# Which two of three accumulator banks share a PSUM tile: the up projection's units of seven in a hybrid transformer layer

## The chip, the core and the metric

The kernel runs on one core of a Trainium2 chip. It computes one layer of a diffusion backbone in fp32, with matrix products made of three products of rounded parts (`fp32r`). The metric is the device time of one execution in microseconds; the numbers of a kernel are the median of its runs, and one further execution is taken by the profiler.

Engines are named as the profile names them: PE is TensorE (matmuls; PEld is its weight load), DVE is VectorE, ACT is ScalarE, POOL is GpSimd, SP the queue that issues most DMAs.

## The reference

The layer is adaLN modulation, neighbourhood attention and bidirectional retention, a merge, an output projection, and then an MLP with a depthwise convolution over tokens. The change lies in the MLP's first half:

```python
def _conv_ffn(h, w_up, conv_w, conv_b, w_down):
    u = h @ w_up                                   # (1024, 1024) @ (1024, 5632)
    up = jnp.pad(u, ((0, 0), (pad, pad), (0, 0)))
    u = sum(up[:, i:i + n] * conv_w[i] for i in range(CONV_W)) + conv_b
    a, val = jnp.split(u, 2, axis=-1)
    return (jax.nn.silu(a) * val) @ w_down
```

`w_up` has 2 x 2816 columns: a gate half and a value half, each in 22 blocks of 128. A block `j` of the gate and block `j` of the value belong together, since they meet in `silu(a) * val`.

## The kernel before

**The units.** The up projection goes block by block in 22 units. The first two are plain: eight products of 128 columns by 512 tokens for gate and value. The other twenty are units of seven (class `Up`, a `Seven`): gate and value block are the two rows of a 2 x 2 block matrix, the two halves of the input features its columns, and the input `h` is split likewise into two feature halves and two token halves, B11, B21, B12, B22. Seven products in place of eight then give the four results (gate or value, token half); for that, weights are summed beforehand (`load`, four sums on POOL, L1401 to L1404) and inputs too (T1 to T4, ready in SBUF). A product is twelve matmuls of 128x512 (`prod`, L1387): four feature blocks by the three combinations of rounded high and low parts. Before it, ACT rounds the weight (L1412) and DVE makes the low part (L1413).

Each unit accumulates in three banks of PSUM, X, Y and Z, 512 fp32 columns each:

| step | input | bank | after it |
|---|---|---|---|
| 0 | B11 (`h2a`) | X, opened | p1 = copy of X, ACT, L1433 |
| 1 | T2 | Y, opened | u2 = Y + p1, DVE, L1436 |
| 2 | T1 | Z, opened | |
| 3 | T3 | Y, added to | u3 = Y + p1, DVE, L1442; then the add of result (1,1) = Z + u3, DVE, L1423 |
| 4 | B21 (`h2a`) | X, added to | result (0,0) = copy of X, ACT, L1851 |
| 5 | T4 | Y, added to | the add of result (1,0) = Y + p1, DVE, L1423 |
| 6 | B22 (`h2h`, `h2l`) | Z, added to | the add of result (0,1) = Z + u2, DVE, L1423; then the unit's convolution |

The convolution (`conv`) of a unit has for gate (`ta`) and value (`at`) a scaled copy on ACT (L1784) and two taps on DVE (L1785, L1786), then silu (L1787, ACT) and a product (L1788, DVE). For every second unit POOL then makes four sums of its outputs (L1802).

**The tiles.** `u_tile` gives a PSUM tile of two banks. There are two pools of two such tiles; the units use the pools in turn, and a unit takes both tiles of its pool. Of its four banks it uses three: before the change X and Y are the two halves of the first tile, and Z is the first half of the second. The kernel is written in a framework that adds the waits between engines itself, from the tiles that each instruction reads and writes, and that may put a ready instruction ahead of its place in the program.

**The order.** Two units are always under way. `interleaved` sorts the steps by

```python
sorted((7 * i + 2 * k, i, k) for i in range(n0, n) for k in range(7))
```

so that between two steps of a unit there is one of its neighbour, and a unit starts just ahead of its predecessor's step 4: (i, 3), (i+1, 0), (i, 4), (i+1, 1), (i, 5), (i+1, 2), (i, 6), (i+1, 3), (i+2, 0), (i+1, 4) and so on. In the first unit of seven, which has no predecessor of its kind, steps 1 and 2 stand in exchanged order before the change. PE and DVE each work through one queue in order.

After the up projection follows the down projection (matmuls of `y` on line 1387), with the tile framework again moving a few of its first matmuls into the end of the stage.

Of the kernel before, what the change touches and what calls it, by code (L numbers as in the profile page):

```python
# [32 lines left out]
NF = FF // P  # L33
# [7 lines left out]
def tile_hybrid_layer(ctx, tc: tile.TileContext, io, dbg=None):  # L41
# [1417 lines left out]
    def interleaved(n0, n):  # L1459
        return [(i, k) for _, i, k in sorted((7 * i + 2 * k, i, k) for i in range(n0, n) for k in range(7))]  # L1460

    class Gates(Seven):
# [17 lines left out]
        def banks(self):  # L1480
            self.X, self.Y, self.Z = (g_ps("u") for _ in range(3))
# [30 lines left out]
    for db in range(KB):  # L1512
# [5 lines left out]
        for half in range(2):  # L1518
# [6 lines left out]
            t = onap.tile([P, 512], F32, tag="pn", bufs=3, name="pnt")  # L1525
# [120 lines left out]
    for kb in range(KB):  # L1646
        t = wop.tile([P, 2, 512], F32R, tag="wo", bufs=KB, name="wo")
# [11 lines left out]
    for kb in (6, 7, 0, 1, 2, 3, 4, 5):  # L1659
        t = (wop if kb >= 6 else op).tile([P, 2, 512], F32R, tag="wx", bufs=2, name="wx") if kb >= 4 else None  # L1660
# [73 lines left out]
    def u_tile(n):  # L1734
        return pu[n // 2 % 2].tile([P, T], F32, tag="u", bufs=2, name="u")
# [70 lines left out]
    def u_out():  # L1806
        return tap.tile([P, T], F32, tag="uu", bufs=4, name="uu")
# [13 lines left out]
    class Up(Seven):  # L1821
# [11 lines left out]

        def banks(self):
            t = u_tile(2 * self.n)
            self.X, self.Y = t[:, 0:512], t[:, 512:1024]
            self.Z = u_tile(2 * self.n + 1)[:, 0:512]
            self.u = [u_out() for _ in range(2)]

        def moving(self, c):  # L1840
# [27 lines left out]
    PLAIN = 2  # L1868
# [11 lines left out]
            combs[f"T{c + 1}"] = comb(c)  # L1880
        conv(j, *us2)
    units[PLAIN + 1].load()
    ups = interleaved(PLAIN, NF)
    ups[1:3] = ups[2], ups[1]
    for i, n in ups:
        units[i].step(n)
    pu[1].release()
    pu[0].release()
# [231 lines left out]
def build(nc, arrays):  # L2120
    io = {k: nc.dram_tensor(f"in_{k}", a.shape, mybir.dt.from_np(a.dtype), kind="ExternalInput").ap() for k, a in arrays.items()}
    io["out"] = nc.dram_tensor("out_0_dram", (T, D), F32, kind="ExternalOutput").ap()
    with tile.TileContext(nc) as tc:
        tile_hybrid_layer(tc, io)
# [11 lines left out]
```

## Time and profile before

| | |
|---|---|
| runs | 1733.86, 1733.59, 1732.75 us: median 1733.59 |
| profiled execution | 1731.98 us, of it 1729.9 us span from the first to the last instruction |
| granted PE clock over the span | 0.999 |
| PE, DVE, ACT, POOL busy, share of the span | 98%, 75%, 49%, 30% |
| units of seven | from 1126.4 to 1513.2 us of the span |
| matmuls in them | 1680 (20 units of 7 products of 12) |

How to read it. A row of the timeline gives the start in us from the span's start, the length in us, engine, line, operation, what it writes and reads, shape and count (rows of equal instructions that follow each other are merged). A matmul is listed with 0.39 us, but matmuls are pipelined and start at a closer pitch, so an engine row of PE that is busy all the time may still hide lost time: the pitch tells. An entry `a <- b: 3.7, 9, 0.6` of the waits says that `a` stood idle for 3.7 us in all, nine times, at most 0.6, until `b` was done. A row of the busy times by stretch has the stretch, its length, then busy time and count of PE, PEld, DVE, ACT and POOL, the clock, and the share and rate of the DMAs.

### The profile page before, as it was taken

What the parts mean: (1) busy time and instruction counts of PE and PEld (TensorE: products, weight loads), DVE (VectorE), ACT (ScalarE), POOL (GpSimd) and SP (SyncE); (2) the same over time, 40 slices, a digit from 0 to 9 for tenths busy, and PEclk for the clock granted to TensorE, in tenths of its full rate; (3) what the DMA queues carried; (4) which work ended last, traced back from release to release, by engine and by line L of the source; (5) the groups of instructions that cost most, each with busy time, mean ns of one, the idle gap of its engine ahead of it and who ended that gap; (6) DMA issues with size and microseconds to landing.
All of it is one profiled execution on the core that took longest, in us unless ns stands there. A gap on an engine that the chain in (4) does not pass through costs nothing.

```text
span 1729.9 us, 24670 instructions
## 1 busy us (share of the span) xinstructions
PE 1701.1 (98%) x8318; PEld 1416.1 (82%) x8318; DVE 1296.3 (75%) x2502; ACT 842.0 (49%) x1794; POOL 523.0 (30%) x443
## 2 busy tenths in 40 slices
PE   7999999999999999999999999999999999999998
PEld 4888888888888888888888888888888888888886
DVE  6578887766777776887665557888998998875757
ACT  7656666553353434544443333644444444554444
POOL 2100000002334243055413300265555555211444
PEclk9999999999999999999999999999999999999999
DMA  9243344343342323668568633732233332586754
GB/s 353 89 132 115 110 128 132 120 146 96 92 122 67 101 64 97 209 230 270 187 219 286 220 139 137 267 112 96 92 94 119 118 96 92 181 293 193 241 156 177
DMA packets 157998, 267.66 MB, mean 155 GB/s; under 512 B 26064, under 2 KB 46768, under 8 KB 157872
## 3 DMA queue, kind: packets, MB, share of 16 engines
q1 hardware_dynamic: 139952, 245.12, 43.5%
q10 hardware_dynamic: 17920, 20.98, 3.4%
q8 instruction: 65, 1.06, 0.3%
q14 instruction: 61, 0.50, 0.1%
HBM read 191.80 MB, written 71.61 MB: 152 GB/s over the span
## 4 chain that ended last, share of the span: by engine, by line
PE 46%; issue 5%; DVE 5%; POOL 3%; ACT 1%; DMA 1%; POOLq 0%; SPq 0%; ACTq 0%; DVEq 0%
PE u L1387 26%; PE y L1387 6%; PE pr L113 2%; PE pr L114 2%; PE pr L112 2%; PE om L124 1%; PE om L123 1%; PE om L125 1%; DVE wc L1413 1%; PE pn L114 1%; PE pn L112 1%; PE pn L113 1%; PE u L113 1%; PE u L114 1%; PE u L112 1%
## 5 line engine op out<-in xcount | busy, mean ns | idle before, releaser
L1387 PE MATMUL u<-T,wc 128*128 128x512 f32 x960 | 225.7, 391 | 0.5 <-ACT pu L1433 0.3
L1387 PEld LDWEIGHTS u<-T,wc 128*128 128x128 f32 x960 | 179.4, 188 | 41.2 <-ACT pu L1433 3.7
L1387 PE MATMUL y<-wc,ahl 128*128 128x512 f32 x924 | 210.1, 389 | 0.4 <-DVE wc L89 0.4
L1387 PEld LDWEIGHTS y<-wc,ahl 128*128 128x128 f32 x924 | 173.4, 188 | 36.8 <-DVE wc L89 0.8
L113 PE MATMUL mm<-low,wc 128*128 128x512 f32 (+1 forms) x320 | 121.4, 379 | 0.0
L1387 PE MATMUL u<-h2a,wc 128*128 128x512 f32 x480 | 112.8, 390 | 0.9 <-DVE pu L1442 0.8
L89 DVE TENSOR_TENSOR wc<-ur,wc 128x512 fp32r<-128x512 f32 x77 | 63.3, 823 | 61.4 <-ACT wc L88 61.4
L1387 PEld LDWEIGHTS u<-h2a,wc 128*128 128x128 f32 x480 | 90.0, 188 | 20.3 <-DVE pu L1442 1.2
L112 PE MATMUL mm<-hx,wc 128*128 128x512 f32 x256 | 103.8, 405 | 0.0
L114 PE MATMUL mm<-hx,wc 128*128 128x512 f32 x256 | 102.9, 402 | 0.0
L1412 ACT CAST wc<-s 128x512 fp32r<-128x512 f32 x80 | 49.7, 622 | 91.0 <-PE u L1387 88.8
L125 PE MATMUL mm<-wc,low 128*128 128x512 f32 (+1 forms) x240 | 91.4, 381 | 0.0
L1387 PE MATMUL u<-hxT,wc 128*128 128x512 f32 x384 | 89.6, 389 | 0.0
L1539 POOL TENSOR_TENSOR col<-col,bcol 128x32 f32<-128x32 f32 x1 | 0.3, 252 | 291.4 <-issue 291.4
L88 ACT CAST wc<-ur 128x512 fp32r<-128x512 f32 x77 | 47.8, 620 | 79.5 <-PE y L1387 74.5
L1413 DVE TENSOR_TENSOR wc<-s,wc 128x512 fp32r<-128x512 f32 x80 | 84.8, 1060 | 1.0 <-ACT wc L1412 0.6
L1387 PEld LDWEIGHTS u<-hxT,wc 128*128 128x128 f32 x384 | 72.1, 188 | 15.0
L89 DVE TENSOR_TENSOR wc<-raw,wc 128x512 fp32r<-128x512 f32 x93 | 63.6, 691 | 22.8 <-ACT wc L88 22.4
L88 ACT CAST wc<-raw 128x512 fp32r<-128x512 f32 x93 | 57.2, 620 | 46.7 <-DMA raw<-in_w_pret 7.7
L123 PE MATMUL mm<-wc,hx 128*128 128x512 f32 x192 | 75.2, 392 | 0.6 <-ACT r L1088 0.6
L124 PE MATMUL mm<-wc,hx 128*128 128x512 f32 x192 | 75.2, 392 | 0.0
L1413 DVE TENSOR_TENSOR wc<-wr,wc 128x512 fp32r<-128x512 f32 x55 | 55.0, 1006 | 17.6 <-ACT wc L1412 15.5
(397 smaller groups left out, 4711.1 us busy)
## 6 DMA issues: line engine op xcount, KB each, us to landing
ur<-in_w_up SPq DMA_DIRECT2D x80, 256.0 KB
ur<-d_a SPq DMA_DIRECT2D x77, 256.0 KB
aw<-in_w_ada SPq DMA_DIRECT2D x32, 512.0 KB
pj<-in_w_down SPq DMA_DIRECT2D x44, 256.0 KB
d_w<-pj SPq DMA_DIRECT2D x44, 256.0 KB
d_a<-sa SPq DMA_DIRECT2D x44, 256.0 KB
ur<-d_w SPq DMA_DIRECT2D x44, 256.0 KB
d_a<-at SPq DMA_DIRECT2D x33, 256.0 KB
```

Source lines behind the costliest of these rows:

```text
L88: act.copy(hi, src)
L89: (lo_eng or vec).tensor_tensor(lo, src, hi.bitcast(F32), ALU.subtract)
L112: pe.matmul(out, wh, xh, start=k == 0, stop=False)
L113: pe.matmul(out, wh, xl, start=False, stop=False)
L114: pe.matmul(out, wl, xh, start=False, stop=k == n - 1)
L123: pe.matmul(out, ah, bh, start=first, stop=False)
L124: pe.matmul(out, ah, bl, start=False, stop=False)
L125: pe.matmul(out, al, bh, start=False, stop=last)
L1387: pe.matmul(out, a, b, start=first and n == 0, stop=last and n == 2, skip_group_check=True)
L1412: pin(act.copy(w[:, 0], a))
L1413: pin(vec.tensor_tensor(w[:, 1], a, w[:, 0].bitcast(F32), ALU.subtract))
L1539: pool.tensor_tensor(col[:, 16:48], col[:, 16:48], bcol[:, 16:48], ALU.add)
```

## The change

X and Z now share the first tile of a unit, and Y has the second, alone. The first unit of seven takes its steps in the plain order of `interleaved`. Steps, products, sums and DMAs are the same in number and size.

```diff
         def banks(self):
             t = u_tile(2 * self.n)
-            self.X, self.Y = t[:, 0:512], t[:, 512:1024]
-            self.Z = u_tile(2 * self.n + 1)[:, 0:512]
+            self.X, self.Z = t[:, 0:512], t[:, 512:1024]
+            self.Y = u_tile(2 * self.n + 1)[:, 0:512]
             self.u = [u_out() for _ in range(2)]
...
     units[PLAIN + 1].load()
-    ups = interleaved(PLAIN, NF)
-    ups[1:3] = ups[2], ups[1]
-    for i, n in ups:
+    for i, n in interleaved(PLAIN, NF):
         units[i].step(n)
```

PE's queue, where one unit (first tile 12756) is about to take step 4 and the next (first tile 12902) has begun. The rows with 12909 as weight are step 0 of the next unit, those with 12925 step 4 of this one, those with T10 and T11 the start of step 1 of the next. Before:

```order
L1387 MATMUL u_12902<-h2a_11094,wc_12909 128x512 x3
L1387 MATMUL u_12902<-h2a_11095,wc_12909 128x512 x3
L1387 MATMUL u_12756<-h2a_11096,wc_12925 128x512 x3
L1387 MATMUL u_12756<-h2a_11097,wc_12925 128x512 x3
L1387 MATMUL u_12756<-h2a_11098,wc_12925 128x512 x3
L1387 MATMUL u_12756<-h2a_11099,wc_12925 128x512 x3
L1387 MATMUL u_12902<-T10_12147,wc_12941 128x512
L1387 MATMUL u_12902<-T11_12148,wc_12941 128x512
```

The same place with the change:

```order
L1387 MATMUL u_12902<-h2a_11094,wc_12909 128x512 x3
L1387 MATMUL u_12902<-h2a_11095,wc_12909 128x512 x3
L1387 MATMUL u_12903<-T10_12147,wc_12941 128x512
L1387 MATMUL u_12903<-T11_12148,wc_12941 128x512
L1387 MATMUL u_12903<-T10_12147,wc_12941 128x512
L1387 MATMUL u_12756<-h2a_11096,wc_12925 128x512 x3
L1387 MATMUL u_12756<-h2a_11097,wc_12925 128x512 x3
L1387 MATMUL u_12756<-h2a_11098,wc_12925 128x512 x3
L1387 MATMUL u_12756<-h2a_11099,wc_12925 128x512 x3
L1387 MATMUL u_12903<-T10_12147,wc_12941 128x512
L1387 MATMUL u_12903<-T11_12148,wc_12941 128x512
```

Three matmuls of the next unit's step 1 have come ahead of this unit's step 4; the other nine follow it. Step 1 writes a tile of its own now (12903), where it wrote the tile of step 0 (12902). It is so in seventeen of the twenty units.

DVE's queue at the same place, as a difference (rows without a sign are the same in both). The first row is the previous unit's last add, L1442 is u3 of this unit, and the last row the add of its result (1,1):

```order
-L1423 TENSOR_TENSOR uu_12599<-u_12598,pu_12602 128x512
+L1423 TENSOR_TENSOR uu_12599<-u_12597,pu_12602 128x512
 L1413 TENSOR_TENSOR wc_12973<-s_12894,wc_12973 128x512
 L1785 SCALAR_TENSOR_TENSOR ta_12859<-uu_12599,cw_12079,ta_12859 128x1023
-L1442 TENSOR_TENSOR pu_12762<-u_12756,pu_12760 128x512
+L1442 TENSOR_TENSOR pu_12762<-u_12757,pu_12760 128x512
 L1786 SCALAR_TENSOR_TENSOR ta_12859<-uu_12599,cw_12079,ta_12859 128x1023
-L1423 TENSOR_TENSOR uu_12759<-u_12757,pu_12762 128x512
+L1423 TENSOR_TENSOR uu_12759<-u_12756,pu_12762 128x512
```

DVE's order does not change, only the tiles that it reads: of the tile 12756, which step 4 writes, the reader was u3 (L1442) and is now the add two places behind it (L1423).

## The prediction

> **What bounds the kernel now.** I read the page first: busy times, then the chain that ended last.
>
> ```profile
> span 1729.9 us, 24670 instructions
> PE 1701.1 (98%) x8318; PEld 1416.1 (82%) x8318; DVE 1296.3 (75%) x2502; ACT 842.0 (49%) x1794; POOL 523.0 (30%) x443
> PE u L1387 26%; PE y L1387 6%; PE pr L113 2%; PE pr L114 2%; PE pr L112 2%; PE om L124 1%; PE om L123 1%; PE om L125 1%; DVE wc L1413 1%; PE pn L114 1%; PE pn L112 1%; PE pn L113 1%; PE u L113 1%; PE u L114 1%; PE u L112 1%
> ```
>
> TensorE bounds it, and its largest piece of the chain is the u products of line 1387. Time can be lost or won only where PE stands still there. For the stage of the units of seven I took the busy times of that stretch, and then its waits.
>
> ```profile
> 1126.30:1513.50 387.20, 385.82 (x1691) 316.00 (x1690) 345.26 (x351) 177.38 (x248) 203.02 (x115) 1.00 0.35 112
> ...
> PEld u L1387 <- ACT pu L1433: 3.7, 9, 0.6
> PEld u L1387 <- DVE pu L1442: 1.2, 1, 1.2
> PEld u L1387 <- DVE pu L1436: 0.3, 1, 0.3
> ```
>
> ```profile
> 1211.19 2.88 PE L1387 MATMUL u<-T,wc 128*128 128x512 f32 x12
> 1213.91 5.60 PE L1387 MATMUL u<-h2a,wc 128*128 128x512 f32 x24
> 1219.35 4.92 PE L1387 MATMUL u<-T,wc 128*128 128x512 f32 x21
> ```
>
> The timeline of PE gives the pitch: 24 matmuls from 1213.91 to 1219.35 are 0.2267 us each, and a product of twelve is 2.72. The stretch's 1691 matmuls need 383.3 of its 387.2 us, so only 3.9 are lost in twenty units. Of these some 1.1 are the last unit's wait for u3 (L1442) and 0.2 the first unit's for u2 (L1436); what is left, 2.6 us, is in the main the wait for p1 (L1433), nine times at most 0.6 on the weight loads. That wait shows how the framework counts: p1 reads bank X, the waiting product of step 1 writes bank Y, and they meet only in that X and Y are one tile. Waits go by tile here, not by bank.
>
> **What the change removes.** Step 1 writes Y, now in a tile of its own, so it no longer waits for p1. Three new waits are covered by products of 2.72 us each. Step 2, writing Z, now waits for p1, but two more products lie between than did for step 1. Step 6, writing Z, waits for ACT's copy of X after step 4, with three products between. Step 1 of the unit after next takes over the tile that the add after step 6 gives back; that add ends at 1212.39 in the rows below, where step 1 starts at 1216.63. Without this cover each would cost PE the copy or add itself, 0.57 to 0.69 us. The gain is at most 2.6 us.
>
> **What it adds.** X and Z share a tile, so step 4, which writes X, now waits for the last reader of Z: the first of the unit's three adds (L1423), the one in step 3. Before, it waited for u3, the reader of Y. On VectorE's unchanged queue the add stands two places behind u3, with a tap of the previous unit's convolution (L1786) between. There are two kinds of unit. Here is one of the earlier kind, beside the PE rows above:
>
> ```profile
> 1211.10 0.68 DVE L1413 TENSOR_TENSOR wc<-ur,wc 128x512 fp32r<-128x512 f32 x1
> 1211.70 0.69 DVE L1423 TENSOR_TENSOR uu<-u,pu 128x512 f32<-128x512 f32 x1
> ...
> 1214.96 0.68 DVE L1442 TENSOR_TENSOR pu<-u,pu 128x512 f32<-128x512 f32 x1
> 1215.56 1.72 DVE L1786 SCALAR_TENSOR_TENSOR ta<-uu,cw,ta 128x1023 f32<-128x1023 f32 x1
> 1217.20 0.68 DVE L1423 TENSOR_TENSOR uu<-u,pu 128x512 f32<-128x512 f32 x1
> ```
>
> Step 4 is the second half of the 24 matmuls: 1213.91 + 2.72 = 1216.63. u3 was done at 1215.64, 1.0 before. The add ends at 1217.88. The change puts three matmuls of step 1 in front of step 4, so PE would reach it at 1216.63 + 0.68 = 1217.31 and stand for 0.57 us. The other kind:
>
> ```profile
> 1191.90 2.88 PE L1387 MATMUL u<-T,wc 128*128 128x512 f32 x12
> 1194.62 5.60 PE L1387 MATMUL u<-h2a,wc 128*128 128x512 f32 x24
> 1200.14 3.74 PE L1387 MATMUL u<-T,wc 128*128 128x512 f32 x15
> ...
> 1199.52 0.57 ACT L1433 COPY pu<-u 128x512 f32<-128x512 f32 x1
> ```
>
> ```profile
> 1191.19 1.78 DVE L1413 TENSOR_TENSOR wc<-ur,wc 128x512 fp32r<-128x512 f32 x1
> 1192.89 0.68 DVE L1423 TENSOR_TENSOR uu<-u,pu 128x512 f32<-128x512 f32 x1
> 1193.49 1.45 DVE L1413 TENSOR_TENSOR wc<-s,wc 128x512 fp32r<-128x512 f32 x1
> 1194.95 1.28 DVE L1785 SCALAR_TENSOR_TENSOR ta<-uu,cw,ta 128x1023 f32<-128x1023 f32 x1
> 1196.15 0.68 DVE L1442 TENSOR_TENSOR pu<-u,pu 128x512 f32<-128x512 f32 x1
> 1196.75 1.71 DVE L1786 SCALAR_TENSOR_TENSOR ta<-uu,cw,ta 128x1023 f32<-128x1023 f32 x1
> 1198.38 0.68 DVE L1423 TENSOR_TENSOR uu<-u,pu 128x512 f32<-128x512 f32 x1
> ```
>
> Step 4 began at 1197.34; the add ends at 1199.06; with the 0.68 put in front PE stands for 1.04 us. This second chain starts when step 6 of the previous unit ends: its last matmul begins a pitch before 1191.90 and lasts 0.39, so 1192.06. Its first add begins 0.83 later, because L1413 beside it took 1.78; in the other kind the same add begins 0.35 after its product.
>
> Two small costs go with each wait. From p1's end (1200.09) to the matmul it released (1200.14) are 0.05 us. And the 15 matmuls that began after that wait took 3.74 us, where 15 at the pitch take 14 x 0.2267 + 0.39 = 3.56: 0.18 at most for restarting, since the next weight load had not run ahead. I take 0.14 for it, 0.19 for both. What stands behind the waiting matmul is the whole of PE: nothing passes it, so each stall is paid in full. No DMA stands among PE's waits in this stage, and ACT and DVE wait for PE more than PE for them, so they move along.
>
> Seventeen units stand in this regular order; the same sum over the rows of the first and the last of them:
>
> ```profile
> 1156.54 5.60 PE L1387 MATMUL u<-h2a,wc 128*128 128x512 f32 x24
> 1463.31 6.01 PE L1387 MATMUL u<-h2a,wc 128*128 128x512 f32 x24
> ...
> 1160.12 0.68 DVE L1423 TENSOR_TENSOR uu<-u,pu 128x512 f32<-128x512 f32 x1
> 1467.72 0.68 DVE L1423 TENSOR_TENSOR uu<-u,pu 128x512 f32<-128x512 f32 x1
> ```
>
> The first gives 1160.80 - (1159.26 + 0.68) = 0.86, the last about 1.4 (its step 4 had already waited 0.3). Eight units give 0.57 and nine some 1.04. Taken as they stand: 8 x 0.76 + 9 x 1.23 = 17.2 us.
>
> The nine may do better. Their extra 0.47 comes from where POOL's sums fall:
>
> ```profile
> 1190.20 2.22 POOL L1401 TENSOR_TENSOR s<-ur 128x512 f32<-128x512 f32 x1 [2.01 <-DVE at L1785]
> 1207.49 1.29 POOL L1401 TENSOR_TENSOR s<-ur 128x512 f32<-128x512 f32 x1 [7.87 <-DVE wc L1413]
> 1207.96 1.90 DVE L1785 SCALAR_TENSOR_TENSOR at<-uu,cw,at 128x1023 f32<-128x1023 f32 x1 [0.60 <-ACT at L1784]
> ```
>
> Beside POOL's L1401 the DVE split takes 1.78, away from it 0.68. If PE stands a microsecond longer per unit while POOL does not, POOL's four convolution sums end earlier against DVE, L1401 falls as in the first kind, on L1785, and all seventeen cost 0.76: 12.9. Between 12.9 and 17.2 I take the middle, 15.0.
> The Trainium skill, SBUF — State Buffer, Who interferes with whom, says that a VectorE instruction with two SBUF inputs and a GpSimd one that reads SBUF exclude each other for a whole instruction; the rows agree (0.68 against 1.78). By that rule the collision is moved to another instruction rather than saved, which is the lower of my two ends.
>
> **The edges.** In the first unit the plain order puts step 3 one product after step 1 instead of a product and four matmuls.
>
> ```profile
> 1134.81 0.68 DVE L1436 TENSOR_TENSOR pu<-u,pu 128x512 f32<-128x512 f32 x1
> 1135.55 3.02 PE L1387 MATMUL u<-T,wc 128*128 128x512 f32 x12
> 1140.83 0.68 DVE L1423 TENSOR_TENSOR uu<-u,pu 128x512 f32<-128x512 f32 x1
> ```
>
> PE would be at step 3 at 1134.56 (1135.55 less four matmuls and the 0.09 it waits); u2 stands behind DVE's backlog until about 1134.9, one split earlier than now, up to 1135.5 if not; then step 4 waits for the add. Bounds 0.5 to 1.5, taken 1.0. The unit before the last has no POOL sums beside it and its add is in time by 0.1 now; bounds 0 to 1.5, taken 0.5. The last unit still waits for u3, by step 5 instead of step 4; the add is over while step 5's nine matmuls run: 0. Everything after it only shifts.
>
> Sum: 15.0 + 1.0 + 0.5 - 2.6 = **+13.9 us**. The profiled execution took 1731.98 (span 1729.9 and 2.1 around it), so 1745.9; the runs' median of 1733.59 lies 1.6 above that execution, so I expect **1747.5** as the median.
>
> **Rivals.**
> - *Chain in time.* If POOL's L1401 leaves this stretch altogether, the first add starts with its product's end: 0.57 - 0.35 = 0.22 per unit, 17 x 0.41 = 7.0, and with the edges and the gain +5.9: 1739.5. For it: DVE is idle before some of these adds. Against: L1401 waits for a DVE split of the same unit and returns to the same place in eight units. 0.12.
> - *Collisions pile up.* All units like the worst row, 1.4 + 0.19: 27, with edges and gain +26: 1759.6. For it: L1785 and L1786 run between 1.28 and 1.9 as POOL falls. Against: a unit that waits also gives DVE time. 0.10.
> - *The wait goes by bank.* Then step 4 would wait only for p1, nothing is added and the 2.6 is won: 1731.0, and 1730.5 without the first unit's present wait of 0.2 and its restart. It decides if the add does not hold up step 4. For it: X and Z are different banks. Against: so are X and Y, and L1433 holds PE up today. 0.04. The Trainium skill, PSUM — Partial Sum Buffer, PSUM bank collisions raise a hardware error, says that two engines on different banks run clean and that guarding by bank is enough; by it neither wait need exist, but the rows show the one that does.
> - *A wash.* DVE and POOL both shift so that what is lost at step 4 equals what step 1 wins: 17 x 0.15 = 2.6, no change, 1733.6. It needs the chain 0.6 us shorter in every unit, more than L1413 can give back in the first kind. 0.04.
>
> **How the numbers follow.** The forecast has 0.70. A measurement of this kernel tells 0.2%, 3.5 us, from no change. Forecast, chain in time and pile-up are all slower by more: 0.92. The wash and most of the bank case (a gain of 2.6 is 0.15%) are within: 0.06; faster by over 0.2%: 0.02. The likeliest case's own range is 1743 to 1753 (12.9 and 17.2 with the edges' bounds); to reach toward the two slower rivals I give 1739 to 1756.
>
> **What would show it.** In the changed profile the waits of the stage should have PEld u on DVE uu L1423 some 18 times, 0.5 to 1.2 us each, 15 to 20 us in all, and L1433 should be gone. PE's timeline should read h2a x12, T x3, then a gap before h2a x12. The stage should take about 401 us for the same matmuls, the products of line 1387 after it the same time as now. If the add ends before the third T matmul, the chain-in-time rival holds; if the gap appears at another step, or L1433 still stands, my reading of the tiles is wrong.

## The result, and the profile after

The changed kernel takes 1746.99 us as the median of its runs (1743.56 to 1747.85), beside 1733.72 us (1731.01 to 1737.54) for the kernel before on the same chip: ratio 1.0077, 95% interval 1.0065 to 1.0088. That is 13.3 us slower, where 1747.5 us and +13.9 were predicted. Two more groups of runs of the same pair gave 1.0074 (1.0062 to 1.0087) and 1.0078 (1.0065 to 1.0091). The profiled execution took 1746.95 us, at a granted clock of 0.999 as before.

First the page: span, busy times, and the lines of the chain of waits.

```profile
span 1744.9 us, 24690 instructions
PE 1702.2 (98%) x8318; PEld 1413.2 (81%) x8318; DVE 1291.2 (74%) x2502; ACT 844.6 (48%) x1794; POOL 522.1 (30%) x443
PE 69%; DVE 14%; issue 6%; DMA 4%; ACT 3%; POOL 3%; SPq 0%; POOLq 0%; ACTq 0%; DVEq 0%
PE u L1387 19%; PE y L1387 6%; PE mm L114 4%; PE mm L112 4%; PE mm L113 4%; PE mm L123 3%; PE mm L124 3%; PE mm L125 3%; DVE wc L1413 2%; PE R L496 2%; DVE uu L1423 2%; DVE at L1785 2%; PE ptp L478 2%; PE pr L114 2%; PE pr L112 2%
```

No busy time tells the difference: PE is busy 1702.2 us, where it was 1701.1, and its share of 98% has not moved. The chain tells it. The products of line 1387 have fallen from 26% to 19% of it, and VectorE's lines of the up projection (L1423, L1413, L1785) stand in the gap.

The stretch of the units of seven, in the busy times by stretch and the waits:

```profile
1126.30:1529.00 402.70, 389.72 (x1694) 316.07 (x1693) 341.29 (x352) 180.19 (x249) 201.58 (x115) 1.00 0.33 108
...
PEld u L1387 <- DVE uu L1423: 18.0, 17, 1.4
PE u L1387 <- DVE uu L1423: 10.8, 17, 1.0
PEld u L1387 <- DVE pu L1436: 1.8, 1, 1.8
...
PEld u L1387 <- ACT pu L1433: 0.5, 1, 0.5
```

Nearly the same matmuls take 402.7 us instead of 387.2. L1433, which headed PE's waits before with nine entries, is down to a single one in the first unit, and in its place stands L1423, the add of result (1,1), seventeen times. The weight load waits 18.0 us for it and the matmul behind it 10.8 us; these are one and the same stalls and are not added. What they cost is read from the starts of the 1680 matmuls. Their pitch, from one start to the next, is 0.2267 us, and whatever two neighbours lie further apart is lost time:

| place | lost before, us | lost after, us |
|---|---|---|
| step 1, regular units (p1) | 2.59 | 0.00 |
| step 4, seventeen regular units | 0.40 | 15.83 |
| first unit, steps 2 and 3 | 0.22 | 2.06 |
| unit before the last, step 4 | 0.00 | 0.04 |
| last unit, steps 4 to 6 | 2.55 | 2.63 |
| of that filled by matmuls of the down projection (six before, seven after) | 1.36 | 1.59 |
| first to last start of the 1680 | 386.4 | 401.2 |

Before the stage (1126.39 and 1126.51 us) and behind it (217.1 and 217.2 us) the two executions agree. All of the change is here, and nearly all of it at step 4. Here is PE's timeline at two regular units of the changed kernel:

```profile
1198.60 2.88 PE L1387 MATMUL u<-h2a,wc 128*128 128x512 f32 x12
1201.32 0.84 PE L1387 MATMUL u<-T,wc 128*128 128x512 f32 x3
1202.91 3.01 PE L1387 MATMUL u<-h2a,wc 128*128 128x512 f32 x12 [0.75 <-DVE uu L1423]
...
1218.68 2.88 PE L1387 MATMUL u<-h2a,wc 128*128 128x512 f32 x12
1221.40 0.84 PE L1387 MATMUL u<-T,wc 128*128 128x512 f32 x3
1222.70 3.02 PE L1387 MATMUL u<-h2a,wc 128*128 128x512 f32 x12 [0.46 <-DVE uu L1423]
```

Step 0 of the next unit, three matmuls of its step 1, a gap, and then step 4. Three matmuls from 1221.40 would let step 4 start at 1222.08; it starts at 1222.70, 0.62 later, and 1201.32 gives 0.91 in the same way. The matmuls after the gap lose another 0.13 before they are at their pitch again (3.02 us for twelve, where step 0 took 2.88). The chain of waits through the second of these gaps, with start, length and what it was:

```profile
1215.86 0.69 DVE wc L1413
1216.55 0.60 DVE uu L1423
1217.15 1.38 DVE wc L1413
1218.53 1.28 DVE ta L1785
1219.81 0.60 DVE pu L1442
1220.41 1.64 DVE ta L1786
1222.05 0.61 DVE uu L1423
1222.66 0.04 issue
1222.70 7.33 PE u L1387 x31
```

From 1215.86 to 1222.66 VectorE works without a pause, and the last of the row is the add that step 4 waits for. So it is not the add's own 0.6 us that counts, nor the two places between u3 and add, but a run of seven VectorE instructions that ends 0.6 us too late.

### The profile page after: what moved, and what is told of

Read it like the earlier page. It is cut to its first block, busy times and chain, and to the rows that moved or that the text cites. A ratio compares the mean times of both kernels' runs of the same rounds, so it can differ in the third digit from the quotient of the medians.

```text
span 1744.9 us, 24690 instructions
## 1 busy us (share of the span) xinstructions
PE 1702.2 (98%) x8318; PEld 1413.2 (81%) x8318; DVE 1291.2 (74%) x2502; ACT 844.6 (48%) x1794; POOL 522.1 (30%) x443
## 4 chain that ended last, share of the span: by engine, by line
PE 69%; DVE 14%; issue 6%; DMA 4%; ACT 3%; POOL 3%; SPq 0%; POOLq 0%; ACTq 0%; DVEq 0%
PE u L1387 19%; PE y L1387 6%; PE mm L114 4%; PE mm L112 4%; PE mm L113 4%; PE mm L123 3%; PE mm L124 3%; PE mm L125 3%; DVE wc L1413 2%; PE R L496 2%; DVE uu L1423 2%; DVE at L1785 2%; PE ptp L478 2%; PE pr L114 2%; PE pr L112 2%
## 5 line engine op out<-in xcount | busy, mean ns | idle before, releaser
L1387 PE MATMUL u<-h2a,wc 128*128 128x512 f32 x480 | 117.5, 394 | 10.8 <-DVE uu L1423 10.8
L89 DVE TENSOR_TENSOR wc<-ur,wc 128x512 fp32r<-128x512 f32 x77 | 62.2, 809 | 61.5 <-ACT wc L88 61.5
L1413 DVE TENSOR_TENSOR wc<-s,wc 128x512 fp32r<-128x512 f32 x80 | 78.8, 985 | 4.0 <-ACT wc L1412 3.7
L89 DVE TENSOR_TENSOR wc<-raw,wc 128x512 fp32r<-128x512 f32 x93 | 63.6, 692 | 24.0 <-ACT wc L88 23.6
L1413 DVE TENSOR_TENSOR wc<-ur,wc 128x512 fp32r<-128x512 f32 x60 | 54.9, 915 | 25.2 <-ACT wc L1412 25.2
```

What stands on the lines that cost most here:

```text
L89: (lo_eng or vec).tensor_tensor(lo, src, hi.bitcast(F32), ALU.subtract)
L1387: pe.matmul(out, a, b, start=first and n == 0, stop=last and n == 2, skip_group_check=True)
L1413: pin(vec.tensor_tensor(w[:, 1], a, w[:, 0].bitcast(F32), ALU.subtract))
```

## The experiments

All kernels were timed beside the kernel before on the same chip; "lost" is counted as in the table above. Each expectation stands as it was put down ahead of its run.

### The edits one by one

The change has two edits. This kernel has the new tiles alone; the first unit keeps steps 1 and 2 exchanged.

```diff
             t = u_tile(2 * self.n)
-            self.X, self.Y = t[:, 0:512], t[:, 512:1024]
-            self.Z = u_tile(2 * self.n + 1)[:, 0:512]
+            self.X, self.Z = t[:, 0:512], t[:, 512:1024]
+            self.Y = u_tile(2 * self.n + 1)[:, 0:512]
```

> Only the tiles are changed (X and Z share, Y alone); the first unit keeps steps 1 and 2 exchanged. Theory (each step waits for the last reader of its tile): the seventeen regular units lose the same 15.8 us at step 4 as in the changed kernel and the 2.6 us at step 1 are won. In the first unit step 3 waits 0.2 us for u2 as before, but step 4 then comes only ten matmuls (2.3 us) behind step 3, and the add that it must wait for ended 1.4 us after that place in the trace of before, less 0.45 for two matmuls put in front: about 1.1 us with the restart. Sum 15.8 + 1.1 - 2.6 = +14.3 against before, 1748.0 us, that is not faster than the changed kernel; the plain order would then even be worth 0.5 to 1 us under this pairing. Rival (the two edits add up, and the plain order alone is what the first unit lost): before + 15.8 - 2.6 = +13.2, 1746.9 less what the changed kernel lost in its first unit beyond that, 1745.2.

Measured: 1748.83 us beside 1731.49, ratio 1.0096 (1.0082 to 1.011), +17.3 us. Neither the expected +14.3 nor the rival's number fits. Steps 1 and 4 of the regular units are as in the changed kernel (0 and 15.1 us lost), but the first unit lost 7.4 us: 1.7 at step 1, 4.5 at step 2, 0.3 at step 3 and 0.9 at step 4. The timelines of PE, ACT and DVE there:

```profile
1132.59 6.40 PE L1387 MATMUL u<-T,wc 128*128 128x512 f32 x20 [2.60 <-ACT pu L1433]
...
1130.49 1.06 ACT L1787 ACTIVATE ta<-ta 128x1024 f32<-128x1024 f32 x1 [4.62 <-DVE ta L1786]
...
1119.80 7.60 DVE L89 TENSOR_TENSOR T<-uu,T 128x512 fp32r<-128x512 f32 x7
```

```profile
1132.70:1136.10 3.40, 3.40 (x9) 2.62 (x10) 3.40 (x5) 0.35 (x1) 0.79 (x1) 0.51 0.50 187
```

Step 2 writes Z, in one tile with X, and now waits for p1. In the exchanged order the framework put only four matmuls of step 1 in front of it. p1 stands on ScalarE behind a silu (L1787) that itself waited 4.62 us for VectorE, whose seven splits L89 took 7.6 us here and 4.3 us in the kernel before. Not all of the 4.5 us is that wait: the last row has a clock of 0.51, and in it the matmuls started 0.43 us apart instead of 0.23, which comes to some 1.6 us. The changed kernel's traces show no such stretch in this stage. My sum for this kernel had left p1 out. The rival had no room for it either.

The other edit alone, with X and Y in one tile:

```diff
-    ups = interleaved(PLAIN, NF)
-    ups[1:3] = ups[2], ups[1]
-    for i, n in ups:
+    for i, n in interleaved(PLAIN, NF):
```

> Only the order of the first unit is changed (steps in plain order); X and Y share a tile as before. Theory: step 3 of the first unit stands closer behind step 1, and u2 is behind VectorE's backlog: PE waits 1.4 to 1.9 us there in place of 0.2, once; the other nineteen units keep their waits. +1.2 to +1.8 us against before, 1735.2 us. Rival (the plain order costs nothing by itself, it only looked so because X and Z share): 1733.7 us and no wait over 0.3 us on u2.

Measured: 1731.31 us beside 1731.49, ratio 0.9999 (0.999 to 1.0008): no difference. The rival was right. The framework put four matmuls of step 2 ahead of step 1, so that eight stand between steps 1 and 3; step 3 lost nothing and step 1 lost 0.70 us for p1. In the regular units 2.0 us were lost at step 1 and nothing at step 4, beside 2.6 and 0.4 in the trace of before. Thus the tiles make the whole of the change, and the first unit's loss belongs to tiles and order together.

Whether the 17.3 us were chance was asked again, beside the changed kernel on one chip:

> The changed kernel as it is, for comparison with the others of this group on the same chip: 13 to 15 us more than before.

> The new tiles with the first unit's steps still exchanged, again, beside the changed kernel on the same chip. Theory (with the exchanged order the framework puts step 2 behind only four matmuls of step 1, and step 2 now waits for p1, which stands on ScalarE behind the silu L1787 of the second plain unit, and that waits for VectorE): the first unit loses 4 to 7 us, the changed kernel's 2 us, so it is 2 to 5 us slower than the changed kernel. Rival (the 17 us above before were VectorE's and GpSimd's chance meeting ahead of the stage in that execution): within 1 us of the changed kernel.

Measured: the changed kernel 1746.06 us (1.0078, 1.0065 to 1.0091), the new tiles alone 1747.20 us (1.0086, 1.0072 to 1.01), beside 1731.69. The difference is 1.1 us and the intervals overlap; the first unit lost 2.2 us this time, of it 0.70 at step 2, and 0.8 us in the changed kernel. My 2 to 5 us were too many. What is left is that the plain order is worth something between 0 and 4 us under the new tiles and that the first unit's loss differs between executions (0.8, 1.6 and 2.1 us in the changed kernel's three traces). Of the two traces of the new tiles alone, the first has the longer splits and the 1.6 us of the halved clock, the second neither (its seven splits took 4.3 us). How much of the 4 us of the first group is the order and how much these two stays open.

### Other ways to place three banks

The third possible pair:

```diff
-            t = u_tile(2 * self.n)
-            self.X, self.Y = t[:, 0:512], t[:, 512:1024]
-            self.Z = u_tile(2 * self.n + 1)[:, 0:512]
+            self.X = u_tile(2 * self.n)[:, 0:512]
+            t = u_tile(2 * self.n + 1)
+            self.Y, self.Z = t[:, 0:512], t[:, 512:1024]
```

> The third pairing: Y and Z share a tile, X has its own; the first unit's order as before. Theory (waits go by tile, and what counts is how much PE work stands between the last reader of the tile and the next step that writes it): step 1 no longer waits for p1, step 4 only for p1; the new waits are step 2 for u2 (one product of 2.72 us between), step 5 for the add of (1,1) (5.4 us between) and step 6 for the add of (1,0) (one product between), all of them covered. So 2.6 us are won against before: 1731.1 us, and about 16 us against the changed kernel. Rival (any tile in which an engine reads one bank while PE writes the other costs time, whichever the banks): slower than before by some microseconds, with waits at steps 2, 5 or 6.

And a tile for each bank; the pools of the two plain units are closed and opened anew with one-bank tiles:

```diff
-            t = u_tile(2 * self.n)
-            self.X, self.Y = t[:, 0:512], t[:, 512:1024]
-            self.Z = u_tile(2 * self.n + 1)[:, 0:512]
+            self.X, self.Y, self.Z = (pu[self.n % 2].tile([P, 512], F32, tag=c, bufs=1, name="u") for c in "XYZ")
...
+    pu[1].release()
+    pu[0].release()
+    pu = [ps(f"u_ps{i + 2}", ("right", "left")[i]) for i in range(2)]
     ups = interleaved(PLAIN, NF)
```

> X, Y and Z each in a one-bank tile of their own (the two pools are opened anew after the two plain units); the first unit's order as before. Theory (no two banks are tied together, so only true dependences are left): step 1 does not wait for p1, step 4 only for p1: before less 2.6 us, 1731.1 us, the same as with Y and Z in one tile within 0.5 us. Rival (the wait at step 4 of the changed kernel belongs to the order of the steps and VectorE's queue, not to the shared tile): step 4 still waits, 1740 us or more. If it is slower than the pairing of Y and Z by more than 1 us, opening the pools anew costs something at the first units.

> The kernel with three one-bank tiles again, beside the others on the same chip: 3 to 4.5 us below before, 17 us below the changed kernel; no wait at steps 1, 4, 5 and 6 in any unit, only the first unit's wait for u2, 0.2 to 1.4 us.

Measured: Y and Z together 1729.34 us, ratio 0.9988 (0.9979 to 0.9997), -2.2 us. Three tiles 1727.28 us, ratio 0.9981 (0.9972 to 0.999), -4.2 us, and in the second group 1728.39 beside 1731.69, ratio 0.998 (0.9971 to 0.9989), -3.3 us. Steps 1, 2 and 4 lose nothing in either kernel. In the stage of Y and Z together these are PE's waits, and two rows of its timeline in the last unit; then come the waits of the second run with three tiles:

```profile
PEld u L1387 <- DVE uu L1423: 1.1, 2, 0.9
PEld u L1387 <- DVE pu L1436: 0.3, 1, 0.3
```

```profile
1501.58 0.84 PE L1387 MATMUL y<-wc,ahl 128*128 128x512 f32 x3
1502.90 3.03 PE L1387 MATMUL u<-T,wc 128*128 128x512 f32 x12 [0.48 <-DVE uu L1423]
```

```profile
PEld u L1387 <- DVE pu L1436: 0.6, 1, 0.6
PE u L1387 <- DVE pu L1436: 0.2, 1, 0.2
```

The order of the steps, the VectorE work and the number of banks are those of the kernel before; only which banks are one tile differs, and that moves PE's loss from step 1 to step 4 and away. So the wait goes by tile. The medians of three tiles gain 1 to 2 us more than that of Y and Z together, though the intervals overlap. The traces show 0.85 us of it, in the last unit: there the step between others is missing, so that the new wait of step 5 was not fully covered (0.75 us lost, and 0.1 behind it; nothing with three tiles). Nine matmuls of the down projection fill the rest of the time ahead of steps 5 and 6. In the first unit three tiles lost more, 1.4 and 0.5 us in the two traces, beside 0.2. The kernel with three tiles is faster than both kernels of this case, by a little: 0.2% below before, 1% below the change.

### The cover ahead of step 4

If step 4 is only reached too early, it needs more work in front of it. Here it comes after all twelve matmuls of the next unit's step 1 instead of three. The function that sorts the steps serves an earlier stage too, and the first of two kernels changed the order there as well; the second did so in the up projection alone:

```diff
-    def interleaved(n0, n):
-        return [(i, k) for _, i, k in sorted((7 * i + 2 * k, i, k) for i in range(n0, n) for k in range(7))]
+    def interleaved(n0, n, late4=0):
+        return [(i, k) for _, i, k in sorted((7 * i + 2 * k + late4 * (k == 4), i, k) for i in range(n0, n) for k in range(7))]
...
-    for i, n in interleaved(PLAIN, NF):
+    for i, n in interleaved(PLAIN, NF, 1.5):
```

> The changed kernel as it is, for comparison with the three below on the same chip. Step 4 of the seventeen regular units should again lose 0.75 us in eight units and some 1.05 us in nine; about 13 to 15 us more than before.

> The changed kernel, but step 4 stands behind the whole of the next unit's step 1 in every unit, so that twelve matmuls (2.72 us) cover the wait for the add instead of three (0.68 us). Theory (step 4 of the changed kernel stands still because the add of (1,1) ends 0.6 to 0.9 us too late for it): 2.04 us more of cover is enough in all units, the 15.8 us vanish, the 2.6 us at step 1 stay won: 15 us below the changed kernel, and 0 to 2.6 us below before, 1730 us beside a before of 1731.5. Rival (VectorE as a whole is behind, so that the wait only moves to the next step that needs it, 5 or 6): the gain is less than half, 1740 us or more, with waits on L1423 or L1442 at steps 5 or 6.

> As the kernel with the late step 4, but with that order in the up projection alone (the function that sorts the steps serves an earlier stage too, and there it had been changed as well; in its trace the up projection began 5.4 us later than in before). Theory: no wait at step 4, the stage as in that run (388 us from the first to the last matmul, of it 3.6 lost in the first and 3.7 in the last unit), and the earlier stages as in before: 1731.5 to 1733, that is 0 to 1.5 us from before and 12 to 14 us below the changed kernel. Rival (the late step 4 costs more elsewhere in the up projection): 1737 us again.

Measured: the changed kernel 1744.64 us (1.0074, 1.0062 to 1.0087); with the late step 4 in both stages 1737.68 us, ratio 1.0034 (1.0022 to 1.0046); in the up projection alone 1729.99 us, ratio 0.9988 (0.9979 to 0.9996), 1.7 us below before and 16 below the change. Step 4 lost nothing in any unit of either. The first kernel began its up projection at 1131.80 us of the span, the second at 1126.05; that is 5.7 of the 8 us between the two, lost ahead of the units of seven; another 2.3 were lost in the first unit (3.6 us beside 1.2). In the second, all that is left is at the edges, the first unit's u2 and the last unit's u3:

```profile
PEld u L1387 <- DVE pu L1442: 2.5, 1, 2.5
PEld u L1387 <- DVE pu L1436: 1.3, 1, 1.3
```

So VectorE as a whole is not behind; one instruction of it was asked for 0.6 to 0.9 us too early. The pairing of X and Z is harmless where the steps are set for it.

### What sets the two kinds of unit

The changed kernel loses 0.75 us in eight units and 1.04 to 1.26 in nine, by turns. This kernel leaves out the four sums that GpSimd makes after every second unit, and stores the outputs themselves instead:

```diff
-            prev[c] = wpool.tile([P, 512], F32, tag="raw", bufs=3, name="sa")
-            pool.tensor_tensor(prev[c], x, y, o)
-            sync.dma_start(d_a[c, j], prev[c])
+            prev[c] = x
+            sync.dma_start(d_a[c, j], x)
```

> The changed kernel without the four sums of L1802 on GpSimd that follow every second unit (the outputs themselves are stored in their place, so the result is another); the queues of TensorE and VectorE in this stage are the same as in the changed kernel. Theory (the two kinds of unit differ only in where GpSimd's L1401 falls, which the four sums of L1802 push about): all seventeen units become of one kind, 0.75 us each, 12.8 us instead of 15.8: 3 us below the changed kernel, and step 4's waits no longer alternate. Rival (the alternation belongs to the units themselves, as the odd ones have other convolution work): the waits still alternate between 0.75 and 1.05, no change in time.

Measured: 1741.63 us beside 1731.33, ratio 1.0056 (1.0043 to 1.0068), 3.0 us below the changed kernel on that chip. All seventeen units lost 0.74 to 0.80, 12.9 us in all, where the changed kernel's trace on that chip lost 15.4. Its waits, longest 0.9 where it was 1.4:

```profile
PEld u L1387 <- DVE uu L1423: 15.0, 17, 0.9
```

Where the collision falls is seen in the changed kernel's rows of DVE and POOL, the first three and the sixth of the costlier kind, the others of the cheaper:

```profile
1192.64 1.28 DVE L1785 SCALAR_TENSOR_TENSOR at<-uu,cw,at 128x1023 f32<-128x1023 f32 x1 [0.57 <-ACT at L1784]
1193.96 2.20 DVE L1786 SCALAR_TENSOR_TENSOR at<-uu,cw,at 128x1023 f32<-128x1023 f32 x1
1196.08 0.68 DVE L1413 TENSOR_TENSOR wc<-ur,wc 128x512 fp32r<-128x512 f32 x1
...
1212.72 1.90 DVE L1785 SCALAR_TENSOR_TENSOR at<-uu,cw,at 128x1023 f32<-128x1023 f32 x1 [0.60 <-ACT at L1784]
1214.66 1.28 DVE L1786 SCALAR_TENSOR_TENSOR at<-uu,cw,at 128x1023 f32<-128x1023 f32 x1
...
1193.31 1.77 POOL L1401 TENSOR_TENSOR s<-ur 128x512 f32<-128x512 f32 x1 [1.78 <-issue]
1212.25 1.29 POOL L1401 TENSOR_TENSOR s<-ur 128x512 f32<-128x512 f32 x1 [8.87 <-DVE wc L1413]
```

L1401 meets the second tap in one kind and the first in the other; both taps together take 3.52 and 3.22 us from start to end, and the 0.30 between them is the 0.29 between the two losses.

Then L1401 itself was taken away; the product that used the sum takes one of its two weight blocks as it is:

```diff
-            pin(eng.tensor_tensor(self.s1, self.a21, self.a22, ALU.add))
+            if self.bare:
+                self.s1 = self.a22
+            else:
+                pin(eng.tensor_tensor(self.s1, self.a21, self.a22, ALU.add))
```

> The changed kernel without the sum L1401 on GpSimd in the units of seven (the product that used it takes one of the two weight blocks unsummed, so the result is another); the order of TensorE's matmuls in the regular units is the same. Theory (the taps L1785 and L1786 ahead of the previous unit's last add are 0.6 to 0.9 us longer because L1401 runs beside them, and that delays the whole chain to the add): the two taps take 1.28 us each, the last add starts 0.3 (one kind) to 0.6 us (the other) earlier and then waits only for its product, and step 4 waits some 0.45 us in every unit, 8 us in all: 8 us below the changed kernel. Rival (another GpSimd sum, L1402 or L1403, moves into the place and lengthens the taps as well): no gain or less than 3 us, the taps still 1.7 to 2.2 us.

Measured: 1766.94 us, ratio 1.0206 (1.0192 to 1.022), 22 us slower than the changed kernel, with less work. Step 4 and the matmuls behind it lost 34.6 us, 1.2 in one kind and 1.7 to 4.3 in the other. My expectation was wrong even in its sign. The rival's way was right, and its price too small. The rows of DVE, POOL and PE at a dear unit, and the busy times of a stretch behind its stall (lines behind 1401 are three higher in this kernel):

```profile
1194.56 2.26 DVE L1788 SCALAR_TENSOR_TENSOR at<-uu,cw,at 128x1023 f32<-128x1023 f32 x1 [0.61 <-ACT at L1787]
1196.86 2.19 DVE L1789 SCALAR_TENSOR_TENSOR at<-uu,cw,at 128x1023 f32<-128x1023 f32 x1
1198.97 1.77 DVE L1416 TENSOR_TENSOR wc<-ur,wc 128x512 fp32r<-128x512 f32 x1
...
1194.45 1.29 POOL L1405 TENSOR_TENSOR s<-ur 128x512 f32<-128x512 f32 x1 [1.44 <-DVE wc L1416]
1195.70 2.27 POOL L1406 TENSOR_TENSOR s<-ur 128x512 f32<-128x512 f32 x1
1198.05 2.14 POOL L1407 TENSOR_TENSOR s<-ur,s 128x512 f32<-128x512 f32 x1
...
1206.44 4.61 PE L1387 MATMUL u<-h2a,wc 128*128 128x512 f32 x12 [2.37 <-DVE uu L1426]
```

```profile
1207.50:1210.90 3.40, 3.40 (x10) 2.63 (x9) 1.30 (x2) 0.43 (x1) 0.00 (x0) 0.50 0.72 231
```

Without L1401, GpSimd's next three sums come earlier and run beside both taps and the split behind them: 2.26 + 2.19 + 1.77 = 6.22 us, where the changed kernel has 1.28 + 2.20 + 0.68 = 4.16 in that place. The previous unit's last add starts some 2 us later, and step 4 begins 2.5 us late instead of 0.9. Three of the dear units lost another 1.6 to 1.8 us each: behind the stall the granted clock stands at 0.50 for 3.4 us, and there the matmuls started 0.43 us apart instead of 0.23 (twelve took 4.61 us, where they take 3.02 behind a stall at full clock). That is 5.0 of the 34.6 us. The dear unit between the first two of them stalled as long, 2.43 us idle at 1250.10, and kept its clock, so what makes it fall stays open.

## Why the prediction was right

- **What bounds the kernel**: right. PE's busy time is the same, and all that was lost is time in which it stands still at line 1387.
- **The gain of at most 2.6**: right. The 2.59 us at step 1 are gone, and the kernel with Y and Z together, which does little else, won 2.2. That the number is so exact is luck. With six matmuls of the down projection there are 1685 pitches, 381.9 us, in the 386.4, so 4.4 us and not 3.9 were lost before; and 0.4 of what was left after u3 and u2 had been lost at step 4. The two slips cancel.
- **Waits go by tile**: right, shown by four ways to put the same three accumulators into tiles. The signs were seventeen waits for L1423, 18.0 us in all, and L1433 gone but for one in the first unit; the longest wait is 1.4 us, where 1.2 was the most expected. The rival of a wait by bank would have given 1731.0 us; it is out.
- **Step 4, cheaper kind**: 0.57 + 0.19 = 0.76 predicted, 0.74 to 0.76 measured in all eight; 0.58 until the add's end, 0.04 of handover and 0.13 of restart in the unit shown, each within 0.01 of its term.
- **Step 4, dearer kind**: 1.23 if the collision stayed, 0.76 if it moved as in the other kind; measured 1.04 to 1.26. The collision moved, from the split onto the tap before it, which is 0.3 us worse a place than in the cheaper kind. The middle, 15.0 us, had been taken for want of a reason; 15.8 us were lost, of which 0.4 in one of these units before, so 15.4 were added. That it lies so near is luck. The lower end, 12.9, is what the seventeen cost where the alternation is taken away, 12.9 measured.
- **The first unit**: +1.0 within 0.5 to 1.5 predicted. +1.8 in the profiled execution, +1.4 and +0.6 in the two others. The size holds, the upper bound does not: I had counted u2 alone, and p1 was late for step 2 as well (0.40 us lost there). The rows of PE and DVE show u2 behind a last product of the plain units:

```profile
1129.23 6.01 PE L1387 MATMUL u<-T,wc 128*128 128x512 f32 x24
1136.60 3.02 PE L1387 MATMUL u<-T,wc 128*128 128x512 f32 x12 [1.36 <-DVE pu L1436]
...
1134.73 1.21 DVE L1788 TENSOR_TENSOR at<-ta,at 128x1024 f32<-128x1024 f32 x1
1135.87 0.68 DVE L1436 TENSOR_TENSOR pu<-u,pu 128x512 f32<-128x512 f32 x1
```

- **The unit before the last**: +0.5 predicted, 0.04 measured; its add is in time.
- **The last unit**: 0 predicted; without the matmuls that fill it, 1.19 us were lost before and 1.04 after. The wait went to step 5 as it should.
- **The sum**: 15.4 + 1.8 + 0.0 - 0.1 - 2.6 = +14.5 lost in the trace, and 0.2 for the seventh matmul of the down projection inside the stage; +13.9 predicted. The medians lie 13.3, 13.3 and 14.4 apart in three groups. The sum is nearer than its terms, which missed by +0.4, +0.8, -0.5 and -0.1.
- **The range**: its own terms give the likeliest case +10.8 to +17.6 us, 1744.4 to 1751.2; the 1743 to 1753 of the prediction are wider by 1.4 and 1.8 us that no term gives.

Of the rivals, the chain in time needed L1401 to leave the stretch. It did not, and the experiment without it shows that another sum would take its place. That the collisions pile up, the dearest rival, did not happen here, but it is what happened without L1401: 29.6 us there without the halved clock, where the rival had 27.

## What to carry to other kernels

Where a framework counts waits by tile, put into one tile those buffers whose last readers are done long before the next write to any of them, and count the matmuls that lie between; better a tile each. Take the whole run of instructions that stands in front of the awaited reader on its queue, not the reader alone, and ask at which place the waiting engine asks for it. And a stall on the engine that is busy 98% of the time is invisible in its busy time: it is read from the pitch. The granted clock of the stretch is read with it, since matmuls at half clock look like lost time too.

## What was not expected of the hardware

VectorE and GpSimd slow each other down only in some instructions (L1401 took 1.29 or 1.77 us in the rows above). In the changed kernel's regular stretch (counts, then shortest, median and longest in ns):

```profile
L1423 DVE TENSOR_TENSOR uu<-u,pu x54: 677/682/692, 1141.0 to 1495.5; 128x512 f32<-128x512 f32 x54
L1413 DVE TENSOR_TENSOR wc<-s,wc x72: 676/726/1711, 1140.3 to 1496.2; 128x512 fp32r<-128x512 f32 x72
L1785 DVE SCALAR_TENSOR_TENSOR at<-uu,cw,at x18: 1283/1592/2411, 1152.5 to 1492.1; 128x1023 f32<-128x1023 f32 x18
```

The adds, which read one operand from PSUM, take 0.68 us each time, though 42 of the 54 ran beside a GpSimd sum; the splits and taps, which read both from SBUF, take up to 1.71 and 2.41. This agrees with the Trainium skill, SBUF — State Buffer, section Who interferes with whom, by which the two engines share one pair of ports and VectorE has a second pair to itself. What I had not expected is how far it reaches: a GpSimd sum less in each unit made this kernel 22 us slower, some 5 of them at half clock, and four less in every second unit made it 3 us faster, since the sums that were left then ran beside other VectorE instructions.
